# Gate and up weights in a macaron block: two of four sums of weight halves made by accumulating transfers

## Chip, cores and metric
One core of a Trainium2 chip runs the whole block in one launch. The metric is device microseconds of one execution, taken as the median of several runs. Three runs of the kernel before took 1198.59, 1198.85 and 1199.2 us; the median is 1198.85 us.

## What is computed
The reference is one encoder block on 528 tokens (512 and 16 meta tokens) of width 1024: a half-step feed-forward, a mixer (a gated linear recurrence and an attention side by side), and a second half-step feed-forward. The change touches only the two feed-forwards, of hidden width 2816:

```python
def swiglu(x, w_gate, w_up, w_down):
    return (jax.nn.silu(x @ w_gate) * (x @ w_up)) @ w_down
...
h = h + 0.5 * swiglu(rms_norm(h, ffn1_norm[layer]), ffn1_w_gate[layer], ffn1_w_up[layer], ffn1_w_down[layer])
...
h = h + 0.5 * swiglu(rms_norm(h, ffn2_norm[layer]), ffn2_w_gate[layer], ffn2_w_up[layer], ffn2_w_down[layer])
return h[:, N_META:]
```

All is float32. The kernel gets that accuracy from TensorE by splitting every operand into a high and a low part and summing three products (high by high, high by low, low by high).

## The kernel before
Weights come as tiles of 128 partitions by 1024 columns (512 KB): one tile is 128 output columns of a weight matrix, with the 1024 inputs in eight blocks of 128. `parted` (L78) splits a loaded tile: ScalarE casts it to `whi` (L84), VectorE subtracts to get `wlo` (L85). The parts lie in two buffers each of the pool `wts` and, for some tiles, two of the pool of the feed-forward (`W.extra`).

The 22 hidden tiles of a feed-forward are taken in four groups. The first group of four is multiplied plainly. The other 18 tiles are taken two at a time, as nine *pairs*, three pairs to a group; after a group's pairs come the eight tiles of `wd` that take its hidden part back to `h`. For a pair, gate and up are each a product of a 2 x 2 block matrix, done with seven half-size products in place of eight (the Strassen-Winograd form). This needs four sums of weight halves for gate and four for up. `seven` (L88) makes them. With `E` and `F` the first and second 512 columns, and `r0`, `r1` the two tiles of gate (or of up), it makes seven work items, in this order for gate and up: `first` splits `r0`; `sums` makes `t[E] = r1[E] + r1[F]` (L110) and `t[F] = t[E] + r0[E]` (L111) and splits both; `more` makes `t[E] = r0[E] + r1[E]` on GpSimd (L116) and `t[F] = t[F] + r0[F]` (L117) and splits both; `last` splits the `F` halves of the two odd tiles.

`pair` uses them in the order P1 and P2 of gate, P1 and P2 of up (tiles of `first`), P5 and P6 of gate and of up (`sums`), P7 of gate, P7 of up, P3 of gate, P3 of up (`more`), P4 of gate and of up (`last`). Each is 12 matmuls (L374) of 264 columns in the first feed-forward and 256 in the second. Products share PSUM banks: P7 of up adds onto the bank of P6 of up, so ScalarE must first have copied that out (L392); P4 of gate adds onto the bank of P7 of gate, which VectorE must have added out (L395).

A scheduler orders each engine's instructions once, when the program is built. Each engine then runs its list in order, and an instruction that waits holds up all behind it. Weight loads are issued by SyncE (SP), which also runs in order.

Of the kernel before, what the change touches and what calls it, by code (L numbers as in the profile page):

```python
# [6 lines left out]
F32 = mybir.dt.float32  # L7
# [4 lines left out]
ALU = mybir.AluOpType  # L12
# [3 lines left out]
P = 128  # L16
# [35 lines left out]
class Weights:  # L52
# [35 lines left out]
    def seven(self, tiles):  # L88


        nc, add, st = self.nc, self.nc.vector.tensor_tensor, {}
        E, F = slice(0, 512), slice(512, 1024)

        def load(key, where, bufs):
            st[key] = where.tile([P, 1024], F32, name="raw", tag="raw", bufs=bufs)
            nc.sync.dma_start(out=st[key], in_=tiles[key])

        def first(i):
            if not i:
                load(0, self.pool, 2)  # L100
                load(2, self.pool, 2)
            self.parted(self.pool, [(slice(0, 1024), st[2 * i])])

        def sums(i):
            if not i:
                load(1, self.extra, 3)
                load(3, self.extra, 3)
            t, r0, r1 = self.extra.tile([P, 1024], F32, name="sums", tag="sums", bufs=2), st[2 * i], st[2 * i + 1]
            st["s", i] = t
            add(t[:, E], r1[:, E], r1[:, F], ALU.add)  # L110
            add(t[:, F], t[:, E], r0[:, E], ALU.add)  # L111
            self.parted(self.extra, [(slice(0, 1024), t)])

        def more(i):
            t, r0, r1 = st["s", i], st[2 * i], st[2 * i + 1]
            nc.gpsimd.tensor_tensor(t[:, E], r0[:, E], r1[:, E], ALU.add)  # L116
            add(t[:, F], t[:, F], r0[:, F], ALU.add)  # L117
            self.parted(self.pool, [(slice(0, 1024), t)])

        def last():  # L120
            self.parted(self.extra, [(E, st[1][:, F]), (F, st[3][:, F])])

        return [lambda i=i, f=f: f(i) for f in (first, sums, more) for i in range(2)] + [last]

    def fill(self):
# [8 lines left out]
class Interleave:  # L134
# [7 lines left out]
    def add(self, gen):  # L142
        self.chains.append([gen, 0.0, None])
# [964 lines left out]
```

## Time and profile before
| | us |
|---|---|
| median of three runs | 1198.85 |
| profiled execution | 1199.99 |
| its span | 1198.1 |
| TensorE busy | 1169.3 |
| VectorE busy | 853.7 |
| ScalarE busy | 581.4 |
| GpSimd busy | 186.1 |

The span is the time between the first and the last instruction of the profiled execution; 1.9 us lie around it. "Busy" is the time in which an engine had an instruction at work. TensorE's matmuls are pipelined, so that a matmul shown as 0.28 us long starts 0.12 us after the one before it; whether TensorE lost time is read from the idle time put down in front of an instruction, and from the distance of starts.

### The profile page before, as it was taken

How to read it: one execution, taken by the hardware profiler on the slowest of the kernel's cores; microseconds unless marked ns; L12 is line 12 of the kernel's file. 1: busy time of each engine (PE TensorE's matmuls, PEld its weight loads, DVE VectorE, ACT ScalarE, POOL GpSimd, SP SyncE). 2: the span in 40 equal slices, each digit the busy share in tenths (PEclk: the TensorE clock that was granted, in tenths of full speed). 3: DMA queues.
4: the chain of work that ended last, by engine and by line, in shares of the span. 5: the costliest groups of instructions: out<-in, count | busy, mean ns of one | idle time of the engine just before them, and what ended most of it. 6: DMA issues, size and time to landing. Idle time of an engine off the chain costs nothing.

```text
span 1198.1 us, 19412 instructions
## 1 busy us (share of the span) xinstructions
PE 1169.3 (98%) x7765; PEld 1070.7 (89%) x7765; DVE 853.7 (71%) x1349; ACT 581.4 (49%) x982; POOL 186.1 (16%) x153
## 2 busy tenths in 40 slices
PE   8999999999999999899999999999999999999998
PEld 8999999999999788878888788888878998998997
DVE  7988848847956769687677835454788956866863
ACT  5545525524645476656547533334444633543541
POOL 1001001001102023233232410122001101101100
PEclk9999999999999999999999999999999999999999
DMA  6133322323223221111111113232413232333213
GB/s 233 63 95 128 102 89 89 114 80 106 71 67 119 81 71 36 53 37 53 36 54 36 62 45 114 85 117 90 156 53 128 97 102 97 109 98 110 89 54 123
DMA packets 34235, 106.22 MB, mean 89 GB/s; under 512 B 3937, under 2 KB 4321, under 8 KB 34145
## 3 DMA queue, kind: packets, MB, share of 16 engines
q1 hardware_dynamic: 33984, 104.44, 26.0%
q8 instruction: 61, 1.00, 0.3%
q0 software_dynamic: 160, 0.54, 0.1%
q14 instruction: 30, 0.24, 0.1%
HBM read 102.87 MB, written 2.10 MB: 88 GB/s over the span
## 4 chain that ended last, share of the span: by engine, by line
PE 86%; DVE 8%; ACT 2%; issue 2%; DMA 1%; SPq 0%; POOL 0%; ACTq 0%; DVEq 0%
PE mm L197 34%; PE mm L374 14%; PE at L374 9%; PE at L197 5%; PE am L197 5%; PE gs L374 4%; PE S L197 4%; PE am L374 2%; DVE wlo L85 2%; PE gs L888 2%; PE S L695 1%; PE mm L734 1%; PE mm L942 1%; PE at L719 1%; ACT whi L84 1%
## 5 line engine op out<-in xcount | busy, mean ns | idle before, releaser
L84 ACT CAST whi<-raw 128x1024 fp32r<-128x1024 f32 (+2 forms) x220 | 189.4, 862 | 290.5 <-PE mm L197 125.8
L85 DVE TENSOR_TENSOR wlo<-raw,whi 128x1024 fp32r<-128x1024 f32 (+2 forms) x220 | 223.5, 1018 | 28.8 <-ACT whi L84 23.1
L197 PE MATMUL mm<-xh,whi 128*128 128x512 f32 (+1 forms) x504 | 166.3, 363 | 4.7 <-ACT xh L278 1.4
L197 PE MATMUL mm<-xl,whi 128*128 128x512 f32 (+1 forms) x504 | 160.3, 352 | 1.3 <-DVE xl L279 1.3
L197 PE MATMUL mm<-xh,wlo 128*128 128x512 f32 (+1 forms) x504 | 159.4, 350 | 0.0
L116 POOL TENSOR_TENSOR sums<-raw 128x512 f32<-128x512 f32 x36 | 57.9, 1609 | 494.8 <-DVE wlo L85 494.8
L84 ACT CAST whi<-sums 128x1024 fp32r<-128x1024 f32 x72 | 75.4, 1050 | 62.4 <-DVE sums L111 21.2
L85 DVE TENSOR_TENSOR wlo<-sums,whi 128x1024 fp32r<-128x1024 f32 x72 | 87.5, 1217 | 25.2 <-ACT whi L84 25.1
L197 PEld LDWEIGHTS mm<-xh,whi 128*128 128x128 f32 x504 | 89.6, 191 | 17.5 <-ACT tm L623 1.8
L197 PEld LDWEIGHTS mm<-xh,wlo 128*128 128x128 f32 x504 | 89.3, 190 | 12.7 <-issue 0.2
L197 PEld LDWEIGHTS mm<-xl,whi 128*128 128x128 f32 x504 | 89.3, 190 | 11.8 <-DVE xl L279 2.2
L875 POOL TENSOR_TENSOR Z<-Z,tot 128x512 f32<-128x512 f32 x32 | 47.3, 1477 | 157.8 <-PE gs L888 125.1
L197 PE MATMUL mm<-hh,wlo 128*128 128x256 f32 (+1 forms) x218 | 63.0, 334 | 0.0
L197 PE MATMUL mm<-hh,whi 128*128 128x256 f32 (+1 forms) x218 | 62.9, 333 | 0.1
L197 PE MATMUL mm<-hl,whi 128*128 128x256 f32 (+1 forms) x218 | 62.9, 332 | 0.0
L374 PE MATMUL mm<-xl,whi 128*128 128x264 f32 (+1 forms) x216 | 61.3, 284 | 0.0
L374 PE MATMUL mm<-xh,whi 128*128 128x264 f32 (+1 forms) x216 | 61.2, 284 | 0.0
L374 PE MATMUL mm<-xh,wlo 128*128 128x264 f32 (+1 forms) x216 | 61.2, 283 | 0.0
L468 DVE SCALAR_TENSOR_TENSOR h<-mm,h 128x512 f32<-128x512 f32 (+2 forms) x40 | 20.9, 544 | 41.6 <-PE mm L197 41.6
L877 DVE TENSOR_TENSOR Z<-Z,tot 128x528 f32<-128x528 f32 (+1 forms) x32 | 32.5, 1014 | 13.4 <-PE gs L888 9.9
L374 PE MATMUL at<-xh,whi 128*128 128x264 f32 (+1 forms) x144 | 42.0, 291 | 0.0
L197 PEld LDWEIGHTS mm<-hh,wlo 128*128 128x128 f32 x218 | 37.2, 188 | 4.5 <-DVE wlo L85 0.7
(365 smaller groups left out, 3376.8 us busy)
## 6 DMA issues: line engine op xcount, KB each, us to landing
raw<-in_wg SPq DMA_DIRECT2D x43, 512.0 KB, 3.6
raw<-in_wu SPq DMA_DIRECT2D x43, 512.0 KB, 3.3
raw<-in_w_in SPq DMA_DIRECT2D x42, 512.0 KB, 3.2
raw<-in_wd SPq DMA_DIRECT2D x48, 384.0 KB, 3.1
raw<-in_wd SPq DMA_DIRECT2D x16, 256.0 KB, 2.6
raw<-in_wup SPq DMA_DIRECT2D x16, 256.0 KB, 2.6
raw<-in_wout SPq DMA_DIRECT2D x8, 512.0 KB, 3.5
h<-in_xT SPq DMA_DIRECT2D x4, 528.0 KB, 6.5
```

Of the source, the lines that this page charges most:

```text
L84: nc.scalar.copy(hi[:, c], src)
L85: nc.vector.tensor_tensor(lo[:, c], src, hi[:, c].bitcast(F32), ALU.subtract)
L116: nc.gpsimd.tensor_tensor(t[:, E], r0[:, E], r1[:, E], ALU.add)
L197: pe.matmul(o, a[:, sl], b[:, cols], start=(k == 0 and i == 0), stop=(k == n - 1 and i == 2))
L374: pe.matmul(o, a[:, sl], b[:, kk, :], start=(start and kk == 0 and i == 0), stop=(kk == 3 and i == 2), skip_group_check=True)
L468: dve.scalar_tensor_tensor(h[c][:, cols], o, 0.5, h[c][:, cols], ALU.mult, ALU.add)
L695: pe.matmul(s[:, WIDE][:, cols], st[e][:, c * P:(c + 1) * P], kk[:, cols], start=(i == 0), stop=(i == 1))
L719: pe.transpose(o[:, k, :], pr[:, k * P:(k + 1) * P], ident)
L734: pe.matmul(av, v[:, k, :], p[:, k, :], start=(k == 0 and i == 0), stop=False)
L875: pool.tensor_tensor(xx, xx, first, ALU.mult)
L877: dve.tensor_tensor(y, y, second, ALU.mult)
L888: pe.matmul(s[:, c, :], ks[:, c * P:(c + 1) * P], ap(Z, T + c * P, ((2 * m, P // (2 * m)), (T + m, 2), (1, m))), start=True, stop=True)
```

## The change
Two of the four sums are made by the transfers themselves. A helper `total(dst, a, b)` loads `a` into `dst` with a plain transfer issued by SP, and then adds `b` to it with an accumulating transfer issued by GpSimd's queue. The second waits until the first has landed. In this way come `t[E] = r1[E] + r1[F]` of `sums` and `r0[E] + r1[E]` of `more`, the latter into a tile of its own (`more`, two buffers). The odd tiles are not loaded whole any more; their `F` halves come in a tile `last` (two buffers).

```diff
+        def total(dst, a, b):
+            nc.sync.dma_start(out=dst, in_=a)
+            nc.gpsimd.dma_start(out=dst, in_=b, accum_op=ALU.add)
         def first(i):
             if not i:
                 load(0, self.pool, 2)
                 load(2, self.pool, 2)
+                for k in range(2):
+                    r1 = tiles[2 * k + 1]
+                    st["s", k] = self.extra.tile([P, 1024], F32, name="sums", tag="sums", bufs=2)
+                    total(st["s", k][:, E], r1[:, E], r1[:, F])
             self.parted(self.pool, [(slice(0, 1024), st[2 * i])])
         def sums(i):
             if not i:
-                load(1, self.extra, 3)
-                load(3, self.extra, 3)
-            t, r0, r1 = self.extra.tile([P, 1024], F32, name="sums", tag="sums", bufs=2), st[2 * i], st[2 * i + 1]
-            st["s", i] = t
-            add(t[:, E], r1[:, E], r1[:, F], ALU.add)
+                for k in range(2):
+                    st["m", k] = self.extra.tile([P, 512], F32, name="more", tag="more", bufs=2)
+                    total(st["m", k], tiles[2 * k][:, E], tiles[2 * k + 1][:, E])
+                st["l"] = self.extra.tile([P, 1024], F32, name="last", tag="last", bufs=2)
+                for k in range(2):
+                    nc.sync.dma_start(out=st["l"][:, k * 512:k * 512 + 512], in_=tiles[2 * k + 1][:, F])
+            t, r0 = st["s", i], st[2 * i]
             add(t[:, F], t[:, E], r0[:, E], ALU.add)
             self.parted(self.extra, [(slice(0, 1024), t)])
         def more(i):
-            t, r0, r1 = st["s", i], st[2 * i], st[2 * i + 1]
-            nc.gpsimd.tensor_tensor(t[:, E], r0[:, E], r1[:, E], ALU.add)
+            t, r0 = st["s", i], st[2 * i]
             add(t[:, F], t[:, F], r0[:, F], ALU.add)
-            self.parted(self.pool, [(slice(0, 1024), t)])
+            self.parted(self.pool, [(E, st["m", i]), (F, t[:, F])])
         def last():
-            self.parted(self.extra, [(E, st[1][:, F]), (F, st[3][:, F])])
+            self.parted(self.extra, [(slice(0, 1024), st["l"])])
```

After the change the lines of `seven` are L100 (plain half), L101 (accumulating half), L122 (was L111), L127 (was L117); lines behind `seven` are 10 higher (L374 is L384, L392 is L402).

GpSimd in the first feed-forward, second and third pair, before: four additions, `sums_1307` and `sums_1340` being gate and up of the second pair, `sums_1559` and `sums_1592` of the third.

```order
L116 TENSOR_TENSOR sums_1307<-raw_1205,raw_1303 128x512 [waits DMAHW6_49,DVE_49,Pool_49]
L116 TENSOR_TENSOR sums_1340<-raw_1207,raw_1305 128x512 [waits DMAHW0_49,DMAHW7_49,DVE_49,Pool_49]
L116 TENSOR_TENSOR sums_1559<-raw_1457,raw_1555 128x512 [waits DMAHW1_49,DMAHW2_49,DVE_49,Pool_49]
L116 TENSOR_TENSOR sums_1592<-raw_1459,raw_1557 128x512 [waits DMAHW3_49,DMAHW4_49,DVE_49,Pool_49]
```

After, the same place of GpSimd's list (`sums_1216`, `sums_1219`, `more_1316`, `more_1319` are the second pair's, the others the third's):

```order
L101 DMA more_1316<-in_wg1 128x512 [waits DMAHW4_49,DMASW2_49,DVE_49]
L101 DMA sums_1216<-in_wg1 128x512 [waits DMASW0_49,DMAHW5_49,DVE_49,Activation_49]
L101 DMA sums_1219<-in_wu1 128x512 [waits DMAHW7_49,DMASW1_49,DVE_49]
L101 DMA more_1319<-in_wu1 128x512 [waits DMAHW0_49,DMASW3_49]
L101 DMA more_1575<-in_wg1 128x512 [waits DMAHW4_49,DMASW4_49,DVE_49]
L101 DMA sums_1475<-in_wg1 128x512 [waits DMAHW5_49,DMASW5_49,DVE_49]
L101 DMA more_1578<-in_wu1 128x512 [waits DMAHW7_49,DMASW7_49,DVE_49]
L101 DMA sums_1478<-in_wu1 128x512 [waits DMAHW0_49,DMASW6_49,DVE_49]
```

Each waits for a plain load (DMAHW) into the same tile, and the plain load in turn waits for the tile of the pair before to be free.

ScalarE in the first feed-forward, from the second pair to the third, before: `sums_1559` is the third pair's, all else the second's.

```order
L389 COPY g_1300<-mm_1295 128x264 [waits PE_49]
L84 CAST whi_1437<-raw_1303 128x512 [waits PE_49]
L392 COPY g_1299<-mm_1293 128x264 [waits PE_49]
L84 CAST whi_1437<-raw_1305 128x512 [waits DMAHW0_49]
L389 COPY u_1302<-gs_1298 128x264 [waits PE_49,Activation_49]
L84 CAST whi_1562<-sums_1559 128x1024 [waits DVE_49,PE_49,Activation_49]
L392 COPY u_1301<-at_1296 128x264 [waits PE_49]
```

After, the same place (`sums_1475` is the third pair's):

```order
L399 COPY g_1313<-mm_1308 128x264 [waits PE_49]
L84 CAST whi_1453<-last_1322 128x1024 [waits PE_49]
L402 COPY g_1312<-mm_1306 128x264 [waits PE_49]
L399 COPY u_1315<-gs_1311 128x264 [waits PE_49,Activation_49]
L84 CAST whi_1585<-sums_1475 128x1024 [waits DMASW1_49,DVE_49,PE_49]
L402 COPY u_1314<-at_1309 128x264 [waits PE_49]
```

The cast of the next pair's `sums` still stands ahead of the copy that P7 of up needs, and now waits for a software-queue transfer (DMASW) too. Of the 12 passages from one pair to the next within a group this order stands in all 12 before; after, it stands in 7 (five in the first feed-forward, two in the second), and in the other 5 the copy comes first.

TensorE at the start of the first pair of the first feed-forward, before (`whi_978` gate, `whi_1009` up of `first`, `whi_1058` gate of `sums`):

```order
L374 MATMUL mm_1041<-b11l_294,whi_978 128x264
L374 MATMUL mm_1041<-b11h_293,wlo_979 128x264
L374 MATMUL at_1044<-b11h_293,whi_1009 128x264
L374 MATMUL at_1044<-b11l_294,whi_1009 128x264
L374 MATMUL am_1045<-b21h_295,whi_1009 128x264
L374 MATMUL am_1045<-b21l_296,whi_1009 128x264
L374 MATMUL mm_1041<-n2h_299,whi_1058 128x264
L374 MATMUL mm_1041<-n2l_300,whi_1058 128x264
L374 MATMUL at_1044<-b11h_293,wlo_1010 128x264
L374 MATMUL at_1044<-b11h_293,whi_1009 128x264
L374 MATMUL at_1044<-b11l_294,whi_1009 128x264
L374 MATMUL mm_1042<-b21h_295,whi_978 128x264
```

After (`whi_984` gate, `whi_1015` up):

```order
L384 MATMUL mm_1047<-b11l_294,whi_984 128x264
L384 MATMUL mm_1047<-b11h_293,wlo_985 128x264 [waits DVE_49]
...
L384 MATMUL mm_1048<-b21h_295,whi_984 128x264 [waits DVE_49]
L384 MATMUL mm_1048<-b21l_296,whi_984 128x264
L384 MATMUL mm_1048<-b21h_295,wlo_985 128x264
...
L384 MATMUL at_1050<-b11h_293,whi_1015 128x264 [waits Activation_49]
L384 MATMUL at_1050<-b11l_294,whi_1015 128x264
L384 MATMUL at_1050<-b11h_293,wlo_1016 128x264 [waits DVE_49]
```

The 12 matmuls of P2 of gate now stand ahead of the first matmul of up.

## Rows read from the trace of the kernel before

**Rows 1.** Page: busy time by engine; DMA queue (packets, MB, share of 16 engines).

```profile
PE 1169.3 (98%) x7765; PEld 1070.7 (89%) x7765; DVE 853.7 (71%) x1349; ACT 581.4 (49%) x982; POOL 186.1 (16%) x153
...
q1 hardware_dynamic: 33984, 104.44, 26.0%
```

**Rows 2.** Windows, a pair each: us, PE, PEld, DVE, ACT, POOL busy, clock, DMA.

```profile
120.22:140.80 20.58, 20.58 (x172) 20.58 (x171) 17.70 (x25) 11.29 (x19) 2.95 (x2) 1.00 0.31 98
...
948.00:968.30 20.30, 20.30 (x171) 20.30 (x171) 17.21 (x25) 11.12 (x19) 3.51 (x2) 1.00 0.28 93
```

**Rows 3.** Lines: the weight sums; busy us, mean ns, idle before.

```profile
L116 POOL TENSOR_TENSOR sums<-raw 128x512 f32<-128x512 f32 x36 | 57.9, 1609 | 494.8 <-DVE wlo L85 494.8
...
L117 DVE TENSOR_TENSOR sums<-sums,raw 128x512 f32<-128x512 f32 x36 | 38.3, 1064 | 0.0
...
L110 DVE TENSOR_TENSOR sums<-raw 128x512 f32<-128x512 f32 x36 | 34.8, 967 | 3.1 <-DMA raw<-in_wu 2.4
```

**Rows 4.** Timeline, TensorE: start, us, instruction, [idle before, releaser].

```profile
86.25 0.39 PE L374 MATMUL at<-b11h,whi 128*128 128x264 f32 x1 [1.26 <-ACT whi L84]
...
87.51 0.39 PE L374 MATMUL at<-b11h,wlo 128*128 128x264 f32 x1 [0.25 <-DVE wlo L85]
...
186.33 0.39 PE L374 MATMUL at<-b11h,wlo 128*128 128x264 f32 x1 [0.66 <-DVE wlo L85]
...
284.14 0.39 PE L374 MATMUL at<-b11h,wlo 128*128 128x264 f32 x1 [0.70 <-DVE wlo L85]
```

**Rows 5.** Timeline, ScalarE, VectorE and GpSimd, just ahead of these waits.

```profile
85.16 1.04 ACT L84 CAST whi<-raw 128x1024 fp32r<-128x1024 f32 x1 [2.08 <-DMA raw<-in_wu]
...
184.01 2.27 DVE L85 TENSOR_TENSOR wlo<-raw,whi 128x1024 fp32r<-128x1024 f32 x1
...
183.89 1.30 POOL L116 TENSOR_TENSOR sums<-raw 128x512 f32<-128x512 f32 x1 [4.16 <-DVE wlo L85]
```

**Rows 6.** Timeline, ScalarE, second pair of the first feed-forward.

```profile
109.31 1.05 ACT L84 CAST whi<-sums 128x1024 fp32r<-128x1024 f32 x1
...
117.78 1.05 ACT L84 CAST whi<-sums 128x1024 fp32r<-128x1024 f32 x1 [0.96 <-PE at L374]
118.73 0.37 ACT L392 COPY u<-at 128x264 f32<-128x264 f32 x1
```

**Rows 7.** Timeline, TensorE, the same pair: first and last matmul of P7 gate, P7 up.

```profile
117.66 0.28 PE L374 MATMUL mm<-xh,whi 128*128 128x264 f32 x1
...
118.98 0.28 PE L374 MATMUL mm<-xh,wlo 128*128 128x264 f32 x1
119.16 0.39 PE L374 MATMUL at<-xh,whi 128*128 128x264 f32 x1
```

**Rows 8.** Timeline, VectorE, the same pair.

```profile
109.52 0.70 DVE L273 TENSOR_TENSOR hl<-u,hh 128x528 fp32r<-128x528 f32 x1
110.14 1.79 DVE L117 TENSOR_TENSOR sums<-sums,raw 128x512 f32<-128x512 f32 x1
111.85 0.41 DVE L386 TENSOR_TENSOR g<-g,mm 128x264 f32<-128x264 f32 x1
112.19 1.21 DVE L85 TENSOR_TENSOR wlo<-sums,whi 128x1024 fp32r<-128x1024 f32 x1
...
114.16 0.69 DVE L111 TENSOR_TENSOR sums<-sums,raw 128x512 f32<-128x512 f32 x1
...
116.25 1.29 DVE L85 TENSOR_TENSOR wlo<-raw,whi 128x512 fp32r<-128x512 f32 x2
```

**Rows 9.** DMA: 256 KB loads; the pairs' loads (L96); GpSimd's two 264 KB loads.

```profile
raw<-in_wd SPq DMA_DIRECT2D x16, 256.0 KB, 2.6
...
DMA to landing us min/median/max: 3.0/3.3/7.1
...
DMA to landing us min/median/max: 3.1/3.2/3.3
```

**Rows 10.** Timeline at the start: SP's load of the fifth tile, ScalarE's cast of it.

```profile
21.09 0.33 SPq L72 DMA_DIRECT2D raw<-in_wg  x1
...
29.44 1.05 ACT L84 CAST whi<-raw 128x1024 fp32r<-128x1024 f32 x1 [3.90 <-PE S L197]
```

## Prediction
> **What bounds the kernel now.** I read the busy times first, then the windows of single pairs, then TensorE's idle time, and last who is late there. TensorE is busy 1169.3 us of a span of 1198.1 us, VectorE 853.7, GpSimd 186.1 [rows 1]. The reader is to see that the engines which the change relieves are not the ones that end anything: a pair of the first feed-forward lasts 20.58 us with TensorE busy all of it, VectorE 17.70, GpSimd 2.95 [rows 2]. So the only thing to be won is idle time of TensorE inside the pairs. There are just four such waits in the 18 pairs: 1.26 and 0.25 us at the first pair, 0.66 and 0.70 us in the first pairs of the next two groups, 2.87 us in all [rows 4]. The second feed-forward has none.
>
> What to look at next is how close the engines come to being late elsewhere. Between P7 of gate and P7 of up the matmuls start 0.18 us apart in place of 0.12, and then 0.22 [rows 7]: P7 of up waits, a tenth of a microsecond long, for the copy at 118.73, which stands behind the cast of the next pair's `sums` at 117.78 [rows 6]. That cast is let go by TensorE (its buffer is free when P6 of up has ended), so today the sums have no part in it. But there is no slack behind it.
>
> **What the change removes.** On VectorE 36 additions of 0.97 us, on GpSimd 36 of 1.61 us [rows 3]; per pair 1.9 us and 3.2 us. Beside that, VectorE loses the time in which it is held up by GpSimd: `wlo` took 2.27 us at 184.01 where GpSimd's addition began at 183.89 [rows 5], against 1.21 us without it [rows 8]. All this lies beside a TensorE that is busy, except at the four waits. The two of 0.66 and 0.70 us end with a `wlo` of that kind: I count them as gone. The 1.26 us are a late load (the cast of up began at 85.16, when its tile had landed) [rows 5]; the new order puts P2 of gate, 12 matmuls or 12 x 0.122 = 1.5 us (20.58 us over 168 matmuls [rows 2]), ahead of the first matmul of up, so this wait and the 0.25 us behind it are filled. Gain: 2.87 us; least 0, if other work is late there.
>
> **What it adds and hides.** ScalarE and VectorE split `more` in two pieces each and `last` in one instead of two: one instruction more per pair and engine, some 0.1 to 0.2 us, beside 9 us in which ScalarE and 3 us in which VectorE is idle [rows 2]. Cost nothing; VectorE is still better off by 1.8 us. Bytes: a pair loads 2 MB today and 3.5 MB then. The queue moved 104.44 MB in 26.0% of 1198.1 us, or 335 GB/s [rows 1]; 1.5 MB more are 4.7 us of the engines per pair, which have 14 us free (DMA share 0.31 [rows 2]). Hidden as bandwidth; what counts is latency. At the start eight halves and four accumulating transfers of the first pairs go out around the load issued at 21.09; its cast at 29.44 waited for TensorE, not for it [rows 10]. With 3.3 us for the landing [rows 9] that leaves 5 us; the added traffic is about 1.8 MB, 5.3 us. Taken as 0, at most 1 us.
>
> **The new wait.** The tile of `sums` is double buffered, gate and up, so a pair's `sums` of gate can be loaded only when the pair before has split its `more`. I follow this through the second pair of the first group. After the split of the sums VectorE's second `hl` lets it go on at 110.14; with GpSimd's hold-up and L117 (now behind) gone, L386 (0.35) and two halves of `wlo` (1.29 for two) follow, until 111.8 [rows 8]. Then SP loads the plain half, 256 KB: 2.6 us [rows 9], 114.4. Then GpSimd, whose list holds only these transfers, issues the accumulating one. Let L be the time from this issue to landing. Then VectorE adds (L122, 0.69 [rows 8]) and ScalarE casts. That cast is the one at 117.78, ahead of the copy for P7 of up. It is late if 111.8 + 2.6 + L + 0.69 > 117.78, that is if **L > 2.7 us**; all beyond is TensorE time, since nothing but P7 of up is next in its list. Queued behind the waiting L122 on VectorE is also the addition that frees the bank for P4 of gate.
>
> This order stands at 7 passages between pairs. At the other 5 the copy comes first; there L122 holds up only the addition ahead of P4 of gate, three products later (119.16 [rows 7] + 36 x 0.122 = 123.5). Less 0.69, the cast 1.05, `wlo` 1.22 and the addition 0.42 [rows 6, 8] it must have landed by 120.1: L up to 5.7 us is free. In the first pairs of a group the sums are made during the products with `wd`, far ahead.
>
> **The size of L.** No row shows an accumulating transfer. From below: the two plain 264 KB loads through GpSimd's queue took 3.1 and 3.3 us from issue to landing [rows 9]; an accumulating one must read the destination as well, so hardly less, though something under 2.7 can't be excluded for 256 KB on an idle queue. From above: the longest landing of a 512 KB load of these tiles, 7.1 us [rows 9]. It is nearest to the plain load of its own queue, 3.2, plus what it moves more: 256 KB read once more, 0.8 us at 335 GB/s. Just ahead of it on the same queue goes the accumulation of `more` of gate (two reads, 1.6 us, with a head start of some 0.7 us): 0.9 us. I take L = 3.2 + 0.8 + 0.9 = 4.9 us.
>
> On this the Trainium skill speaks against the change. "Collectives: The Full Stack", section "The bandwidth ceiling: the fold count and why AG ≠ RS ≠ AR", says that a transfer that adds is slower not through the addition but because it reads two sources on one ring. "DMA: Bandwidth & Descriptors", section "Issuing engines are not separate DMA queues", says that transfers of SP and GpSimd run on the same engines and interleave. By the two together L is the sum above; were each queue its own, the 0.9 us would fall away and the seven passages would cost 6 us less. No row here shows either.
>
> **Sum.** Seven passages x (4.9 - 2.7) = 15.4 us; five passages 0; less 2.87: +12.5 us. On the profiled execution's own 1199.99 us that is 1212.5; the median of the runs lies 1.14 us lower, so **1211.4 us**, slower by 1.0%.
>
> **Rivals.**
> - *The transfers are hidden* (the other side: faster). L is under 2.8, or the tile is free a microsecond sooner than I read. Then no passage waits and the 2.87 us are won: 1196.0 us. For it: the waits it removes are plainly there [rows 4], and the threshold is a sum of six durations read to some tenths. Against: plain loads of that queue already take 3.1. It decides for as long as L stays under 2.7.
> - *A draw.* L between 2.8 and 3.45, near the plain load: 7 x 0.1 to 0.75 less 2.87 is -2.2 to +2.4 us, 1196.7 to 1201.2. It needs the second read and the queue to cost nearly nothing.
> - *The accumulation is the bound.* If adding in the transfer is several times slower than loading, a pair's 1 MB of it fills the queue: 2.5 MB plain take 7.8 us; 1 MB at a quarter of 335 GB/s takes 12.5, together a whole pair. L is then 8 or more, the five loose passages wait too: 7 x 5.3 + 5 x 2.3 - 2.9 = 45.7, 1244.6 us. Nothing shown speaks for a quarter of the rate, nor against it.
> - *VectorE's relief counts for more than the waits shown.* It was busy 17.70 of 20.58 us, and TensorE still had no gap [rows 2]; past the four waits and 12 x 0.1 us at P7 of up there is nothing to take. Less than 1.3 us.
>
> **How the numbers follow.** The forecast's case (L from 3.45 to 7.1) 0.60; with 7.1: 7 x 4.4 + 5 x 1.4 - 2.9 = +34.9, 1233.8. Hidden 0.15, draw 0.13, bound by accumulation 0.12. What a measurement can tell from no change is about 0.2%, 2.4 us: faster 0.15, same 0.13, slower 0.72. The range runs from the hidden case, 1196, to a little beyond the upper bound of L, 1237; the forecast's own case alone is 1201 to 1234.
>
> **What would show it.** Right: idle time ahead of P7 of up at seven passages, about L - 2.7 each, put down to ScalarE's copy L402, with VectorE's L122 waiting for a load of `sums` by GpSimd's queue ahead of it; a row that gives L between 3.5 and 7; no GpSimd additions in the pairs, `wlo` at 1.22 us, and the four waits of before gone. Wrong: pairs of 20.58 and 20.3 us as today, or L122 finding its data there. If TensorE waits at P4 of gate or at a new pair's P1, the loose passages or the loads of `r0` are the bound; if the matmuls themselves are spaced wider than 0.122 us, it is none of this.

## The result, and the profile after

The changed kernel takes 1274.36 us (median of 4 runs, 1272.37 to 1277.38), the kernel before in the same session 1198.72 us (4 runs, 1198.46 to 1199.2): a ratio of 1.0633, 95% interval 1.061 to 1.0655, slower by 75.6 us. The forecast of 1211.4 us had the sign and the place right and the size six times too small; the time lies far outside its range.

The page, in the columns of [rows 1]:

```profile
PE 1189.3 (94%) x7765; PEld 1089.6 (86%) x7765; DVE 807.5 (64%) x1331; ACT 582.7 (46%) x1000; POOL 192.3 (15%) x189
...
q1 hardware_dynamic: 44352, 113.88, 28.3%
q0 software_dynamic: 10528, 19.42, 9.2%
```

VectorE is relieved by 46 us, as the change meant it to be, and nothing comes of it. TensorE does the same 7765 matmuls in 20 us more, so it was not only kept waiting, it was also slower while it worked. q0 is the queue of the accumulating transfers.

Now the two feed-forwards, from the first matmul of their first pair to that of their last product of a pair, and between the two one pair alone, the second. Before (columns as in [rows 2]):

```profile
83.38:342.50 259.12, 256.25 (x2090) 254.69 (x2088) 192.09 (x271) 118.94 (x186) 26.44 (x18) 1.00 0.28 93
...
105.96:126.55 20.59, 20.59 (x170) 20.49 (x169) 19.03 (x27) 11.77 (x20) 2.95 (x2) 1.00 0.29 104
...
913.40:1161.44 248.04, 247.96 (x1800) 235.78 (x1799) 187.22 (x254) 117.87 (x186) 31.50 (x18) 1.00 0.29 96
```

After:

```profile
84.06:382.13 298.07, 266.98 (x2090) 265.01 (x2088) 170.12 (x264) 119.45 (x195) 27.93 (x32) 0.95 0.48 123
...
106.65:137.03 30.38, 22.92 (x171) 22.50 (x169) 18.93 (x29) 13.15 (x23) 3.49 (x4) 0.89 0.50 127
...
953.16:1234.64 281.48, 257.05 (x1801) 243.45 (x1799) 165.70 (x247) 118.43 (x195) 27.93 (x32) 0.96 0.51 130
```

The two stretches grow by 39.0 and 33.4 us, together 72.4 of the 73.5 us by which the span grew; the mixer between them is unchanged. What TensorE does not work in them grows from 2.9 to 31.1 us and from 0.1 to 24.4 us, together 52.6 us; its busy time by 10.7 and 9.1, 19.8 us, at a clock of 0.95 and 0.96 in the mean where it was 1.00. So the loss has two parts, **waits of 52.6 us and slow work of 19.8 us**. The four waits of [rows 4] are gone; the waits that came are 55.5 us. TensorE's waits by who ended them, total, number of times and longest:

```profile
PE at L384 <- ACT u L402: 40.5, 7, 7.0
PE mm L384 <- DVE g L405: 10.5, 5, 4.7
...
PE mm L384 <- DVE wlo L85: 2.6, 3, 1.1
```

The first line is P7 of up, seven times, 5.8 us each, at the seven passages named in the prediction. The second is P4 of gate at the other five. (1.9 us more are P4 of up; the 2.6 us of the last line are P1 of gate of the next pair.) The passage from the second to the third pair, which the prediction worked through, in the four timelines of SP, GpSimd, VectorE and ScalarE, and then TensorE's:

```profile
114.41 0.33 SPq L100 DMA_DIRECT2D sums<-in_wg  x1
```
```profile
117.24 0.87 POOL L101 DMA_DIRECT2D more<-in_wg  x1 [15.98 <-DMA more<-in_wg]
118.97 0.87 POOL L101 DMA_DIRECT2D sums<-in_wg  x1 [0.87 <-DMA sums<-in_wg]
```
```profile
125.52 0.69 DVE L122 TENSOR_TENSOR sums<-sums,raw 128x512 f32<-128x512 f32 x1 [6.46 <-DMA sums<-in_wg]
```
```profile
117.71 0.37 ACT L402 COPY g<-mm 128x264 f32<-128x264 f32 x1
...
126.29 1.04 ACT L84 CAST whi<-sums 128x1024 fp32r<-128x1024 f32 x1 [7.50 <-DVE sums L122]
127.24 0.37 ACT L402 COPY u<-at 128x264 f32<-128x264 f32 x1
```
```profile
127.67 0.59 PE L384 MATMUL at<-xh,whi 128*128 128x264 f32 x1 [6.43 <-ACT u L402]
```

This is the chain that was foreseen, link by link: the plain half waits for its buffer until 114.41, the accumulating half goes out when that has landed (118.97), VectorE adds when this has landed (125.52, behind an idle time of 6.46 us that ends with a DMA), ScalarE casts, and the copy for P7 of up comes behind the cast. [Rows 6] showed the same cast and copy without a gap.

What happens next is the part that was not foreseen. Windows of the changed kernel: the wait, the 4.33 us behind it, and the 4 us after those:

```profile
121.20:127.67 6.47, 0.04 (x2) 0.00 (x1) 0.99 (x2) 1.32 (x2) 1.75 (x2) 0.81 1.06 231
127.67:132.00 4.33, 4.33 (x19) 4.33 (x20) 3.15 (x6) 0.42 (x1) 0.00 (x0) 0.50 0.00 0
132.00:136.00 4.00, 4.00 (x34) 4.00 (x34) 2.65 (x5) 2.75 (x4) 0.00 (x0) 0.99 0.00 0
```

After the wait the granted clock is 0.50 of the full one (1.2 in place of 2.4 GHz): 19 matmuls in 4.33 us, then 34 in 4.00 us. No byte is moved in those 4.33 us, so it is not the memory that slows them. By such windows it is so after the nine waits of 2.26 to 6.99 us in the two stretches, and after none of those up to 1.82 us: 19.8 / 9 = 2.2 us each.

### The profile page after: what moved, and what is told of

Its sections match the earlier page's. It is cut to its first block, busy times and chain, and to the rows that moved or that the text cites. A ratio compares the mean times of both kernels' runs of the same rounds, so it can differ in the third digit from the quotient of the medians.

```text
span 1271.6 us, 19619 instructions
## 1 busy us (share of the span) xinstructions
PE 1189.3 (94%) x7765; PEld 1089.6 (86%) x7765; DVE 807.5 (64%) x1331; ACT 582.7 (46%) x1000; POOL 192.3 (15%) x189
## 3 DMA queue, kind: packets, MB, share of 16 engines
q0 software_dynamic: 10528, 19.42, 9.2%
## 4 chain that ended last, share of the span: by engine, by line
PE 72%; DVE 11%; DMA 10%; ACT 4%; issue 3%; POOL 0%; SPq 0%; ACTq 0%; POOLq 0%; DVEq 0%
PE mm L207 33%; PE mm L384 9%; DMA sums<-in_wg 6%; PE at L384 6%; PE at L207 4%; PE S L207 4%; PE am L207 4%; DVE wlo L85 2%; PE gs L384 2%; ACT whi L84 2%; DMA more<-in_wg 2%; PE gs L898 2%; PE S L705 1%; PE mm L744 1%; PE mm L952 1%
## 5 line engine op out<-in xcount | busy, mean ns | idle before, releaser
L84 ACT CAST whi<-raw 128x1024 fp32r<-128x1024 f32 (+2 forms) x184 | 167.1, 909 | 285.4 <-PE mm L207 128.2
L85 DVE TENSOR_TENSOR wlo<-raw,whi 128x1024 fp32r<-128x1024 f32 (+2 forms) x184 | 194.1, 1055 | 24.6 <-ACT whi L84 20.3
L207 PEld LDWEIGHTS mm<-xh,whi 128*128 128x128 f32 x504 | 90.1, 192 | 18.5 <-ACT xh L288 2.7
L84 ACT CAST whi<-sums 128x1024 fp32r<-128x1024 f32 (+1 forms) x72 | 59.8, 833 | 100.0 <-DVE sums L122 91.2
L101 POOL DMA_DIRECT2D more<-in_wg x18 | 16.6, 922 | 482.8 <-DMA more<-in_wg 327.1
L384 PE MATMUL at<-xh,whi 128*128 128x264 f32 (+1 forms) x144 | 47.0, 326 | 42.4 <-ACT u L402 40.5
L85 DVE TENSOR_TENSOR wlo<-sums,whi 128x1024 fp32r<-128x1024 f32 (+1 forms) x72 | 68.6, 953 | 23.7 <-ACT whi L84 23.6
L384 PE MATMUL mm<-xh,whi 128*128 128x264 f32 (+1 forms) x216 | 65.2, 302 | 10.5 <-DVE g L405 10.5
L122 DVE TENSOR_TENSOR sums<-sums,raw 128x512 f32<-128x512 f32 x36 | 24.8, 688 | 75.6 <-DMA sums<-in_wg 70.9
L384 PEld LDWEIGHTS at<-xh,whi 128*128 128x128 f32 x144 | 31.8, 220 | 44.8 <-ACT u L402 42.0
L384 PE MATMUL mm<-xl,whi 128*128 128x264 f32 (+1 forms) x216 | 64.6, 299 | 0.0
L384 PE MATMUL mm<-xh,wlo 128*128 128x264 f32 (+1 forms) x216 | 64.3, 298 | 0.0
L384 PEld LDWEIGHTS mm<-xh,whi 128*128 128x128 f32 x216 | 44.7, 207 | 11.6 <-DVE g L405 11.6
```

The lines of the kernel that those rows point to most:

```text
L84: nc.scalar.copy(hi[:, c], src)
L85: nc.vector.tensor_tensor(lo[:, c], src, hi[:, c].bitcast(F32), ALU.subtract)
L101: nc.gpsimd.dma_start(out=dst, in_=b, accum_op=ALU.add)
L207: pe.matmul(o, a[:, sl], b[:, cols], start=(k == 0 and i == 0), stop=(k == n - 1 and i == 2))
L384: pe.matmul(o, a[:, sl], b[:, kk, :], start=(start and kk == 0 and i == 0), stop=(kk == 3 and i == 2), skip_group_check=True)
```

## The experiments

Two theories of the waits stood against each other. **A**: the chain starts too late for its length; plain half, accumulating half, addition and cast would do no harm if the buffer came free earlier. **B**: the accumulating transfers are too slow for what a pair asks of them, or their traffic is, wherever they start. For the slow matmuls: a consequence of the waits, or of the traffic (**F**).

**1. The second half written, not added**

```diff
-            nc.gpsimd.dma_start(out=dst, in_=b, accum_op=ALU.add)
+            nc.gpsimd.dma_start(out=dst, in_=b)
```

> The second halves of sums and more go through GpSimd's queue to the same place as now, with the same bytes and the same wait for the first half, but they overwrite it instead of adding to it (this leaves out the addition in two of the four sums). Theory A, a chain of two landings in a burst that fills the DMA engines: part of the 6.4 us of the second landing is the reading and adding of the old values, the rest is the queue in front of it. The second half lands in 4 to 5 us, as the plain halves do in this burst (3.8 to 4.7 us), the seven waits fall from 5.8 us to 3 to 4 us each and fewer of them end in the low clock: 1215 to 1240 us. Rival B, the arithmetic of the accumulation is the whole cost: landing 3 us, 1196 to 1205 us. Rival C, accumulating costs no more than writing and only the burst and the chain count: 1265 to 1275 us.

Measured: 1244.54 us, ratio 1.038 (1.0341 to 1.042). A little above A's upper end, between B's and C's. The halves land in 4.2 and 3.7 us in place of 6.4 and 6.5 (medians of the transfers of sums), the seven waits are 27.7 us (4.0 each) in place of 40.5, and TensorE's busy time in the two stretches is 11.7 us above that of before, in place of 19.8. So the adding itself, in this traffic, is 2.2 to 2.8 us of the landing. Without any adding the seven passages would still wait 4 us: two landings, one behind the other, are too long for that start. The landings of the changed kernel (median us from issue to landing, last column; SPq is the plain half, POOLq the accumulating one), then those of this run:

```profile
sums<-in_wg SPq DMA_DIRECT2D x18, 256.0 KB, 3.8
sums<-in_wu SPq DMA_DIRECT2D x18, 256.0 KB, 4.7
...
sums<-in_wg POOLq DMA_DIRECT2D x18, 256.0 KB, 6.4
sums<-in_wu POOLq DMA_DIRECT2D x18, 256.0 KB, 6.5
```
```profile
sums<-in_wg POOLq DMA_DIRECT2D x18, 256.0 KB, 4.2
sums<-in_wu POOLq DMA_DIRECT2D x18, 256.0 KB, 3.7
```

How busy the adding keeps the DMA engines shows in the queue's line of this run, beside the one above:

```profile
q0 software_dynamic: 5920, 19.42, 4.6%
```

The same 19.42 MB take 4.6% of 16 engines over 1240.3 us here, 57 us or 340 GB/s, and 9.2% over 1271.6 us, 117 us or 166 GB/s, when they are added. The Trainium skill ("Collectives: The Full Stack", section "The bandwidth ceiling: the fold count and why AG ≠ RS ≠ AR") says of a ReduceScatter that it runs at about half the rate of an AllGather, which only copies, because the add needs two source reads; the trace agrees in the factor and does not show the reads.

**2. The second half left out**

```diff
-            nc.gpsimd.dma_start(out=dst, in_=b, accum_op=ALU.add)
```

> The second, accumulating half is left out altogether (the sums are then those of one half only); the plain first half stays where it is. Theory A: the landing that the cast waits for is now the plain half, released at the same place, some 3 us after its issue since the burst is smaller: the cast is at most 1 us late, no wait of TensorE over 1.5 us, clock not lowered: 1195 to 1203 us. Rival C, the burst of plain transfers alone makes the copies late: over 1215 us.

Measured: 1196.94 us, ratio 0.9971 (0.9959 to 0.9983). As A expected. No wait over 0.5 us in the pairs, the stretches last 256.43 and 247.28 us, and that with the cast ahead of the copy at all twelve passages, since ScalarE's order came out as before the change. This is what the change would win if the accumulation took no time, and it is worth 0.29%: the term of 2.87 us for the four waits is confirmed. The plain halves of sums land in 3.8 and 4.1 us here, with no accumulation anywhere near, not in the 2.6 us of a lone load of that size [rows 9]: it is the burst of plain loads (two tiles and six halves) that delays them.

**3. The accumulated half in a tile of its own**

```diff
-                    st["s", k] = self.extra.tile([P, 1024], F32, name="sums", tag="sums", bufs=2)
-                    total(st["s", k][:, E], r1[:, E], r1[:, F])
+                    st["s", k] = self.extra.tile([P, 512], F32, name="sums", tag="sums", bufs=2)
+                    total(st["s", k], r1[:, E], r1[:, F])
...
+            t, r0, u = st["s", i], st[2 * i], self.extra.tile([P, 512], F32, name="sumf", tag="sumf", bufs=2)
+            st["f", i] = u; add(u, t, r0[:, E], ALU.add)
+            self.parted(self.extra, [(E, t), (F, u)])
```

> The accumulated half of sums gets a tile of its own, apart from the half that VectorE makes; the same bytes of on-chip memory, the same transfers and additions. Its slot comes free after the cast of sums and not only after that of more, so the plain half and the accumulating half are issued about one pair of products (some 6 to 10 us) earlier. In this order the cast of the next pair's sums still stands ahead of the copy of up at all twelve passages. Theory A, lateness of a chain that starts too late: the waits of TensorE at P7 go to below 1 us, the clock stays up, 1194 to 1202 us. Rival B/C, the accumulating transfers are too slow for what is asked of them in a pair, wherever they start: above 1230 us. Rival D, the loss is bound to the cast standing ahead of the copy: twelve such places now instead of seven, above 1274 us.

Measured: 1204.35 us, ratio 1.0035 (1.0024 to 1.0046). B and D fall: the same bytes, accumulated in the same queue, with the cast ahead of the copy at all twelve passages, and no wait at P7 of up. At the passage above, SP's plain half and GpSimd's accumulating one go out some 10 us earlier:

```profile
103.85 0.33 SPq L100 DMA_DIRECT2D sums<-in_wg  x1
```
```profile
108.62 0.86 POOL L101 DMA_DIRECT2D sums<-in_wg  x1 [7.46 <-DVE u L412]
```

It stays 2 us above A's upper end. TensorE's order is not the same in this kernel: nine matmuls of the first pair are drawn forward into the plain products of the first group, and there are new waits of 2.4 us (at 31.77, for VectorE), 1.2 (104.82), 2.3 (864.53) and 0.6 us (933.22), 6.5 us against the 2.9 won.

**4 and 5. Only sums, and only more, by accumulating transfer** (the other as before, and the odd tiles loaded whole). Run 4's edit, cut short and written against the changed kernel; run 5 keeps the line taken out here and makes the halves of `sums` on VectorE, as before:

```diff
-                    total(st["m", k], tiles[2 * k][:, E], tiles[2 * k + 1][:, E])
+            nc.gpsimd.tensor_tensor(t[:, E], r0[:, E], r1[:, E], ALU.add)
```

> Only the halves of sums come by accumulating transfer; more is added by GpSimd and the odd tiles are loaded whole, as before. Here the cast of the next pair's sums stands ahead of the copy of up at five of the twelve passages. Theory A: five late copies, somewhat less late because the burst is smaller (4 to 5.5 us each) with 2.5 us more for the clock after each: 1225 to 1245 us. Rival E, the transfers of more and last, not those of sums, make the loss: 1196 to 1206 us.

> Only the halves of more come by accumulating transfer; the halves of sums are added by VectorE and the odd tiles are loaded whole, as before. Theory A: the cast ahead of the copy of up needs no accumulating transfer, and more is wanted half a pair later: no new wait over 1.5 us, 1194 to 1203 us. Rival E, the traffic of any accumulating transfer makes the loss: 1225 us or more.

Measured: sums only 1261.65 us, ratio 1.0534 (1.0491 to 1.0577); more only 1200.57 us, ratio 1.0 (0.9986 to 1.0015). E falls: it is the transfers of sums. More by itself costs nothing and wins nothing, though its accumulating halves land no sooner (4.9 and 6.6 us), since it is wanted half a pair later. Sums only was above what I expected. Its waits:

```profile
PE at L381 <- ACT u L399: 25.0, 5, 6.9
PE mm L381 <- DVE g L402: 13.4, 5, 3.7
PE mm L381 <- DVE wlo L85: 5.5, 5, 2.2
```

Five waits at P7 of up, where ScalarE's order has the cast ahead of the copy in this kernel (not the same passages as in the changed one); at five of the other seven P4 of gate waits, at the last two P1 of the next pair (1.74 and 2.22 us). So in both kernels P7 waits where the cast comes first, and P4 or what follows it where the copy does. But the burst is not smaller with whole odd tiles (accumulating halves land in 6.1 and 6.6 us), and P4 loses 13.4 us.

**6 to 8. Waits of a chosen length, with no transfer**

```diff
+                    with tc.manual_schedule(engines={pe.engine}): us = pair(ft, xq, n)
...
+                    [act.copy(ft.tile([P, 10, nh], U8, name="sink", tag="sink")[:], ap(X, 0, [[0, 10], [1, nh]])) for _ in range(2 if i else 0)]
```

> The kernel before, with TensorE's order in the pairs fixed as written, as a basis for the next two; nothing else is changed. All theories: within 5 us of the kernel before, no fall of the granted clock in the pairs.

> As the basis, but ScalarE copies the bank that P7 of up will write once more, eight times over into a scratch tile, so P7 of up waits some 2.3 us at each of the 18 pairs; no transfer is added. Theory A (a wait of 4 us and more lowers TensorE's clock, one of 2 us does not): 18 x 2.3 = 41 us more than the basis and nothing else, granted clock 1.0 after the waits. Rival F (the slow stretches after the waits come from the DMA traffic and not from the wait): no low clock here and none in the next.

> As the one before, with two such copies of ten times the bank: P7 of up waits some 5.7 us at each of the 18 pairs, with no transfer added. Theory A: after each wait the granted clock reads 0.5 for some 5 us, which costs 2 to 3 us a time: 18 x 5.7 = 103 us for the waits and 36 to 54 us for the clock over the basis. Rival F: 103 us and no low clock.

Measured: 1203.45, 1229.93 and 1319.85 us. The basis is 0.24% above the kernel before (its clock in the first feed-forward is 0.99: against what I expected, it read 0.50 behind a new wait of 2.87 us at 88.84). The short waits became 1.37 us each, as ScalarE had time in hand (24.7 us in 18 waits; the time rose by 26.5); the long ones 4.34 us:

```profile
PE at L374 <- ACT sink L392: 78.1, 18, 4.7
```

The time rose by 116.4 us over the basis, 38 more than these waits. Windows of the basis, of the short and of the long waits: for the last two first the stretch behind the second wait, then the two feed-forwards.

```profile
84.36:346.16 261.80, 257.57 (x2090) 256.25 (x2089) 193.88 (x272) 119.32 (x186) 26.42 (x18) 0.99 0.29 92
917.62:1165.65 248.03, 247.95 (x1800) 235.78 (x1799) 187.16 (x254) 117.85 (x186) 31.48 (x18) 1.00 0.30 96
```
```profile
123.38:128.00 4.62, 4.62 (x38) 4.62 (x39) 3.88 (x7) 1.75 (x3) 0.52 (x1) 1.00 0.00 0
83.33:357.26 273.93, 257.55 (x2089) 254.87 (x2088) 194.87 (x272) 133.97 (x195) 26.34 (x18) 1.00 0.27 87
926.93:1188.74 261.81, 249.59 (x1801) 235.96 (x1800) 191.42 (x254) 132.61 (x195) 27.78 (x18) 1.00 0.29 91
```
```profile
133.59:138.00 4.41, 4.41 (x20) 4.41 (x21) 0.86 (x2) 0.00 (x0) 0.00 (x0) 0.50 0.00 0
84.86:405.54 320.68, 277.22 (x2090) 274.53 (x2089) 195.98 (x272) 158.36 (x204) 26.22 (x18) 0.92 0.23 75
976.90:1282.83 305.93, 267.40 (x1801) 253.77 (x1800) 192.45 (x254) 155.94 (x204) 27.68 (x18) 0.92 0.25 78
```

After the long waits the clock is 0.50 with the DMA engines idle, and TensorE's busy time is 19.7 + 19.5 = 39.1 us above the basis, 2.2 us for each of the 18 waits, as much as in the changed kernel. After the short ones it is 1.00, and the busy times are that of the basis and 1.6 us above it. F falls: the slow matmuls follow from the waits. Waits shorter than the 4 us that I wrote can cost this too, though: after that of 2.26 us in the changed kernel and after 2.55 and 2.82 us in run 10 the clock read 0.50, and even after 1.74 us in run 4 (at 108.33) and 1.88 us in run 9 (at 1068.33). After 2.41 us in run 7 (at 87.36) it stayed at 1.00, so the length of a wait alone does not decide it.

**9. A third buffer for sums**

```diff
-name="sums", tag="sums", bufs=2)
+name="sums", tag="sums", bufs=3)
```

> One line differs from the changed kernel: sums has three buffers in place of two (4 KB more). TensorE's order is the same; a gate tile can now be loaded a whole pair ahead, in the buffer that stands free, and an up tile in the one that gate's tile of the pair before gave back. The cast of the next pair's sums stands ahead of the copy of up at all twelve passages. Theory A (only the late start of the chain makes the loss, and the four removed waits are worth 2.9 us): no wait of TensorE over 1 us in the pairs, clock up, 1194 to 1199 us, ratio to the kernel before 0.996 to 0.999. Rival B (the accumulating transfers cannot keep up with what a pair asks for): above 1215 us. Rival D (the cast ahead of the copy is what costs): above 1274 us. In between, 1200 to 1205 us: new waits as in the kernel with the tile split, from work that is drawn forward.

Measured: 1229.19 us, ratio 1.0255 (1.0231 to 1.0279): more than half of the loss gone, but above what A gave. The gate's tile is early and no P7 of up waits any more, with the cast ahead of the copy at all twelve passages, so D falls again. The up tile takes the buffer that the gate gave back, at the same place as the gate's did, and is late in its stead. VectorE stands behind it with the addition that frees the bank for P4 of gate:

```profile
104.61 0.69 DVE L122 TENSOR_TENSOR sums<-sums,raw 128x512 f32<-128x512 f32 x1 [8.48 <-DMA sums<-in_wu]
105.22 1.22 DVE L85 TENSOR_TENSOR wlo<-sums,whi 128x1024 fp32r<-128x1024 f32 x1
106.35 0.42 DVE L405 TENSOR_TENSOR g<-g,mm 128x264 f32<-128x264 f32 x1
```

P4 of gate waits 21.8 us in 11 waits. The wait moved one link on; I had not followed the second tile.

**10. More's second half left out**

```diff
-total(st["m", k], tiles[2 * k][:, E], tiles[2 * k + 1][:, E])
+nc.sync.dma_start(out=st["m", k], in_=tiles[2 * k][:, E])
```

> The accumulating second half of more is left out (more is then one half only); sums as in the changed kernel, with the same order on ScalarE (copy behind the cast at the same seven passages) and the same start of the chain. This takes away the one accumulating transfer that stands ahead of that of sums in GpSimd's queue. Theory A1 (the landing of 6.4 us is 4 us of its own and 2.4 us behind the accumulation of more): landing 4.0 to 5 us, the seven waits 3.5 to 4.5 us each in place of 5.8, 1225 to 1248 us. Rival A2 (it is the burst of plain loads, not the other accumulation): landing 6 us, 1258 to 1272 us.

Measured: 1254.46 us, ratio 1.0449 (1.0425 to 1.0472). The landing (4.8 and 5.0 us) and the waits (29.7 us in seven, 4.2 each) are those of A1; the time is not, because I let the clock's share shrink with the waits: TensorE's busy time is 19.3 us above before, nearly as much as in the changed kernel. But it does not follow that the accumulation of more is what delays the landing: in run 4, without it and with whole odd tiles, the landing stayed at 6.1 and 6.6 us. Plain loads under way delay it too; how much each kind costs by the byte is not shown.

**11 and 12. The own tile with its pieces in the other order, with two and with four buffers**

```diff
-            self.parted(self.extra, [(E, t), (F, u)])
+            self.parted(self.extra, [(F, u), (E, t)])
...
-name="sums", tag="sums", bufs=2)
+name="sums", tag="sums", bufs=4)
```

> The kernel with the accumulated half in a tile of its own, with the two pieces of the split taken in the other order (VectorE's half first). TensorE's order is then that of the kernel before, where the first split kernel drew products of the first pairs forward. All of the transfers and additions are there. Theory A: no wait over 1 us at P7 of up or P4 of gate, the new waits of the first split kernel (6.5 us in all) gone too, and the 2.9 us of the four removed waits won: 1194 to 1199 us, ratio 0.996 to 0.999. Rival G: the landings of 4 to 6 us are still late at some passages, as the piece that is cast first now needs both the transfer and VectorE's addition: 1203 to 1225 us.

> The same with four buffers of half a tile in place of two (4 KB more than the changed kernel), so that both transfers of sums may start a whole pair ahead. Theory A: if the kernel with two buffers already has no waits, the same time within 0.2%; if it still has some, this one has none, 1194 to 1199 us, ratio 0.996 to 0.999. Rival B (the accumulating transfers cannot keep up with what a pair asks for, however early they start): no better than with two buffers and above 1203 us.

Measured: two buffers 1203.02 us, ratio 1.0021 (1.0009 to 1.0034), above A's figure, with waits of 1.2 and 0.6 us left at P4 of gate; four buffers **1198.94 us, ratio 0.9988 (0.9978 to 0.9998)**, at the upper end of what A expected. With all transfers and additions in it, the last is faster than the kernel before by 1.1 us, and 75 us faster than the changed one. Its queue of accumulating transfers and its windows, the second pair first, then the first feed-forward, the mixer and the second feed-forward:

```profile
q0 software_dynamic: 10528, 19.42, 9.9%
```
```profile
104.25:124.67 20.42, 20.42 (x170) 20.42 (x169) 16.26 (x27) 12.01 (x22) 4.21 (x5) 1.00 0.77 178
82.87:338.21 255.34, 254.63 (x2090) 254.24 (x2088) 172.24 (x281) 121.06 (x211) 25.95 (x30) 1.00 0.55 139
338.21:913.36 575.15, 552.30 (x3115) 473.69 (x3113) 390.33 (x670) 295.56 (x528) 129.65 (x115) 0.99 0.25 79
913.36:1159.99 246.63, 246.63 (x1800) 235.36 (x1799) 168.72 (x264) 119.98 (x211) 26.16 (x30) 1.00 0.56 142
```

The feed-forwards are 3.8 and 1.4 us shorter than before, and the stretch between them 4.3 us longer. In it ScalarE waits 8.61 us for the first sums of the second feed-forward, whose transfers go out in one burst with those of more and last, with a weight's cast queued behind it; TensorE waits 2.2 us for that cast at 860.69, and the clock reads 0.50 for some microseconds behind it. I take it for the same mechanism at another place; no run tested that. Of the 5.2 us in the feed-forwards only 2.2 are waits (one of 0.70 us stands at 86.88 again). The other 3.0 us are matmuls that start closer together, among them the first of P7 of up, which no longer start late behind the copy [rows 7]: the cast ahead of that copy is now one of half a tile.

The profiled execution of run 11 is 3.0 us longer than that of before, and the same stretch holds this and more: its feed-forwards are 3.5 us shorter and 0.9 us longer, the stretch between them is 4.5 us longer, the start 0.9 us (a wait of 2.42 us at 7.79, with 0.50 behind it).

## Why the prediction was wrong

The mechanism, the seven places and the sign were right. The step that failed is the length of the chain from the free buffer to the landed sum: two terms of it were mis-sized, and so the five loose passages were put at 0; and the price of a wait in slow matmuls was missing.

- **The gain of 2.87 us** was right: the four waits are gone, and run 2 won 3.3 us with nothing against it.
- **The release at 111.8** was right. In the profile before, gate's copy in this passage stands at

```profile
115.31 0.37 ACT L392 COPY g<-mm 128x264 f32<-128x264 f32 x1
```

  and after at 117.71, so this passage lies 2.4 us later by waits that came earlier; 114.41 less 2.4 is 112.0. At the other six the buffer is free 3.1 to 4.8 us ahead of gate's copy, where the forecast has 115.31 - 111.8 = 3.5 us.
- **"Then SP loads the plain half, 256 KB: 2.6 us"** failed. The row was that of a load that goes out nearly alone; here it goes out in a burst that the change itself makes. From SP's issue to GpSimd's it is 4.5 us in the mean of the seven passages (3.62 to 4.90): 3.9 us to the landing, and 0.6 us from there until GpSimd issues, for which there was no term. Run 2 shows that plain loads do this to each other.
- **"I take L = 3.2 + 0.8 + 0.9 = 4.9 us"** failed. L is 6.6 us in the mean of the seven (5.1 to 8.2). The transfer by itself was sized well: 3.2 + 0.8 = 4.0 us, and among the shortest is one of 4.1 us (at 128.11 in run 3), against 3.0 us for the shortest that does not add (in run 1). The 0.9 us for what shares the engines should have been 2.6.
- Together: 2.2 + 1.9 + 1.7 = 5.8 us a passage, the mean of the seven waits: 40.5 us in place of 15.4. That it comes out to a tenth is partly luck, as the buffers came free half a microsecond earlier in the mean than the forecast has it.
- **"At the other 5 the copy comes first ... L up to 5.7 us is free"**: the order was right, but the chain was 3.6 us longer than taken, and 15.0 us came from P4 and its neighbours in place of 0.
- **The clock** had no term: 19.8 us. The prediction even listed wider spaced matmuls as a sign that "it is none of this"; they are a price of its waits.
- The sum as it should have been: 40.5 + 15.0 + 19.8 - 2.9 = 72.4 us.
- The rival "the accumulation is the bound" gave 1244.6 us and came nearest, but its reason is not what happens: runs 3 and 12 accumulate the same bytes with at most a short wait. The rivals "hidden" and "draw" fall with L. VectorE's relief is worth about what was said: run 2 won 0.4 us beyond the four waits.

What stays open is which waits of 1.7 to 2.9 us lower the clock, and how much of a landing each transfer beside it costs.

## What to carry to other kernels

A buffer that is both loaded and, later, worked on is given back by its last use; before a load into it becomes a chain of two, give the loaded part a tile of its own or more buffers, and follow every tile that takes turns with it. Size a landing by a row from a burst like the one that the change makes, not by a lone load. And a wait of TensorE of more than 2 us mostly cost 1.7 to 2.2 us more here in slow matmuls (11.7 us over seven waits in run 1, 39.1 over 18 in run 8), so a term per wait belongs in the sum.

## What the runs showed of the hardware that I had not expected

- After TensorE had waited 3.71 to 4.72 us, 18 times in run 8, its clock read 0.50 for some microseconds, with at most 0.02 MB moved meanwhile, and 2.2 us were lost a wait; after the 18 waits of 0.79 to 1.71 us in run 7 it read 1.00.
- An accumulating transfer of 256 KB through GpSimd's queue keeps the DMA engines busy twice as long as the same one without adding (166 against 340 GB/s by the queue's line), but at its shortest it lands only 0.9 us later (3.9 us in run 12, at 953.76, against 3.0 us in run 1, at 332.04). In the burst the difference is 2.2 to 2.8 us.
- In the burst of the changed kernel the plain halves of sums and more take 3.5 to 4.7 us (medians) and those of last 5.7 and 6.8 us; loads of 256 KB for `wd` take 2.7 us.
